# Order edges between the down-projection's weight units and VectorE's additions in a Strassen FFN

## Chip, cores and metric

One core of a Trainium2 chip runs the whole layer as one program. The metric is device time in microseconds (us) of one execution, as the median of several runs. Engines: TensorE (PE; PEld is its weight load), VectorE (DVE), ScalarE (ACT), GpSimd (POOL) and SyncE (SP), whose queue issues most transfers. Each engine takes its instructions in the order of its own queue, and waits at an instruction whose inputs are not there yet.

## What is computed

One layer of a decoder: a modulated norm, an input projection, two kinds of attention, an output projection, and then the FFN, where this change lies:

```python
D_MODEL, SEQ, D_FF = 1024, 1024, 2816
h2 = rmsnorm(x, g_ffn[l]) * (1.0 + sc2) + sh2
gate, up = jnp.split(h2 @ w_gu[l], 2, axis=-1)
x = x + ga2 * ((jax.nn.silu(gate) * up) @ w_down[l])
return rmsnorm(x, g_final)
```

## The kernel before

All arithmetic is float32; a product is made of three matmuls over high and low parts ("h" and "l" tiles) of its operands. The gate and up projections and most of the down-projection use seven products in place of eight (Strassen's scheme), so the operands of a product are sums and differences of blocks.

**The FFN loop** (L1328 to L1357) runs over 22 blocks `f` of 128 columns. In each block `ff_prep` (L1266) loads two pieces of the gate and up weights (L1248, SP), forms four differences of them on GpSimd (L1279, L1280, L1283, L1287), and splits seven operands into high parts on ScalarE (L1241) and low parts on VectorE (L1242). The split operands lie in 20 pages of 512 columns, two for each operand. Seven products follow (`ff_mm`, L1254; twelve matmuls each, L1257 to L1259), in PSUM banks of three kinds: four "mm", two "tp", two "o". VectorE takes the products out of PSUM with seven additions (L1337, L1338, L1340, L1343, L1344, L1347, L1351), ScalarE with one copy (L1336); ScalarE applies silu (L1339, L1348), GpSimd multiplies (L1349, L1352) and sends the two halves of the result to memory (L1350, L1353). The first addition of a block is L1337, into `u2`; L1347, into `u3`, is the sixth.

**The weight units.** Between the blocks the program also prepares the weights of the down-projection for later. There are 40 units (L1295: ten pairs of row blocks by four column pieces). A unit `s` goes through one of three buffers (`wslot`, L1298; tiles `mr0`, `mr1` and `f2`, which the trace shows as mr and f). Its steps: two loads on SP (L1305); two multiplications by the gate on VectorE (L1323, 128x256 each); a store of three of its four parts on SP (L1324); four subtractions in place on GpSimd (L1314 to L1317, 128x128 each), which must wait until that store has read the buffer; a store of the result on SP (L1318); and then the buffer is free for unit `s + 3`.

`w_step(s)` (L1308) writes down three things: the load of unit `s + 1`, the subtractions and second store of unit `s - 1`, and the multiplications and first store of unit `s`. The loop calls `w_step(2f - 2)` ahead of the block's products and `w_step(2f - 1)` behind them, so that units 0 and 1 stand in the text of block 1, units 38 and 39 in that of block 20, and the subtractions of unit 39 in that of block 21. `w_load(0)` stands at the end of block 0.

**What sets the order.** The text of the program is not the order of the queues. When the program is complete, a planner runs it against a time model of its own (`schedule_with_timeline_sim`, L1581): at each step an engine takes, among the instructions that the model says are ready, the one of highest priority, which is the one that stands first in the text (`tc.high_priority` moves some ahead). So an instruction whose inputs are ready early goes into its engine's queue early, however late it stands in the text. The order so found is fixed, and on the chip each engine keeps to it.

**Around the loop.** Ahead of it, `normed`, `turned` and `combined` (L1166 to L1223) make the operands of the FFN, with the last matmuls of the output projection (L367 to L369), transposes (L1187) and splits (L1160, L1161). Behind it stands the down-projection (L1362 on), which reads the units' results back from memory (`w_quarter`, L1408).

Of the kernel before, what the change touches and what calls it, by code (L numbers as in the profile page):

```python
# [15 lines left out]
OP = mybir.AluOpType  # L16
# [52 lines left out]
def hybrid_block(ctx, tc, x, c, w_ada, b_ada, g_attn, w_in, kv_norm_g, w_uk, w_uv, w_out, g_ffn,  # L69
                 w_gu, w_down, g_final, lnm, out, dbg=None):  # L70
    nc = tc.nc
    V, A, G, PE = nc.vector, nc.scalar, nc.gpsimd, nc.tensor

    def pool(stack, name, bufs=1, side=None, **kw):
        if kw.get("space") is None:
            kw["reuse_waits"] = "tile"
        return stack.enter_context(tc.tile_pool(name=name, bufs=bufs, side=side, **kw))
# [18 lines left out]
    def mm_tile(tag="mm"):  # L96
        return ps["pool"].tile([P, 512], F32, name=tag, tag=tag, bufs=ps[tag])
# [498 lines left out]
    for i in range(6):  # L596
        f = 1.0 if i < NV else 2.0
# [546 lines left out]
    def quarters(at, names):  # L1144
        return {n: [at.tile([P, 4, 512], F32R, name=f"A{n}{x}") for x in "hl"] for n in names}

    qA = quarters(pool(qr_ctx, "qR"), ("11", "S2"))
# [103 lines left out]
    def ahead(n):  # L1251
        return tc.high_priority(n) if n else nullcontext()

    def ff_mm(w, a, tag):  # L1254
        p = mm_tile(tag)
        for k in range(4):
            PE.matmul(p, w[1][:, k], a[0][:, k], start=(k == 0), stop=False)  # L1257
            PE.matmul(p, w[0][:, k], a[0][:, k], start=False, stop=False)  # L1258
            PE.matmul(p, w[0][:, k], a[1][:, k], start=False, stop=(k == 3))  # L1259
        return p  # L1260

    def u_tile():
        nu[0] += 1
        return us[nu[0] % 6]

    def ff_prep(f):  # L1266
        b11, b21 = ff_w(f * P)
        b12, b22 = ff_w(DFF + f * P)
        t1, t2, t3, t4 = tsum
        if f == 0:  # L1270
            V.tensor_tensor(t1, b12, b11, op=OP.subtract)
            w1 = page_split(t1)
            V.tensor_tensor(t2, b22, t1, op=OP.subtract)
            G.tensor_tensor(t4, b21, t2, op=OP.subtract)
            w4 = page_split(t4)
            w11 = page_split(b11)
        else:
            w11 = page_split(b11)
            G.tensor_tensor(t1, b12, b11, op=OP.subtract)  # L1279
            G.tensor_tensor(t2, b22, t1, op=OP.subtract)  # L1280
        w2 = page_split(t2)
        w21 = page_split(b21)
        G.tensor_tensor(t3, b22, b12, op=OP.subtract)  # L1283
        w3 = page_split(t3)
        if f > 0:
            w1 = page_split(t1)
            G.tensor_tensor(t4, b21, t2, op=OP.subtract)  # L1287
            w4 = page_split(t4)
        w22 = page_split(b22)
        return w11, w21, w1, w2, w3, w4, w22  # L1290
# [7 lines left out]
    def wslot(s):  # L1298
        return wbuf[s % 3].rearrange("p (u r c) -> p u r c", u=2, r=2), wbuf[s % 3].rearrange("p (a c) -> p a c", c=P)

    def w_load(s):
        if s < len(units):
            j, h = units[s]
            for i, u in enumerate((1, 0)):
                nc.sync.dma_start(wslot(s)[0][:, i], wdn[2 * j:2 * j + 2, :, u * 512 + h * P:u * 512 + h * P + P]  # L1305
                                  .rearrange("r p c -> p r c"))

    def w_step(s):  # L1308
        w_load(s + 1)
        if 1 <= s <= len(units):  # L1310
            j, h = units[s - 1]
            b = wslot(s - 1)[1]
            b12, b22, b11, b21 = [b[:, i] for i in range(4)]
            G.tensor_tensor(b11, b12, b11, op=OP.subtract)  # L1314
            G.tensor_tensor(b12, b22, b12, op=OP.subtract)
            G.tensor_tensor(b22, b22, b11, op=OP.subtract)
            G.tensor_tensor(b21, b21, b22, op=OP.subtract)  # L1317
            nc.sync.dma_start(spill_w[j][:, 3:7, h * P:h * P + P], b)  # L1318
        if s < len(units):
            j, h = units[s]  # L1320
            for i, u in enumerate((1, 0)):
                v = wslot(s)[0][:, i]
                V.tensor_tensor(v, v, gate2[:, u:u + 1, h * P:h * P + P].to_broadcast([P, 2, P]), op=OP.mult)  # L1323
            nc.sync.dma_start(spill_w[j][:, 0:3, h * P:h * P + P], wslot(s)[1][:, 1:4])  # L1324
# [3 lines left out]
    for f in range(NF):  # L1328
        with ahead(PF if f == 0 else 0):
            w11, w21, w1, w2, w3, w4, w22 = ff_prep(f)  # L1330
        if f:
            w_step(2 * f - 2)
        x_, u2, u3, u5 = [u_tile() for _ in range(4)]
        if f == 0:
            p5, p4 = ff_mm(w1, qA["S1"], "tp"), ff_mm(w4, qA["22"], "o")
        A.activation(x_, ff_mm(w11, qA["11"], "mm"), AF.Copy)  # L1336
        V.tensor_tensor(u2, ff_mm(w2, qA["S2"], "tp"), x_, op=OP.add)  # L1337
        V.tensor_tensor(x_, ff_mm(w21, qA["12"], "mm"), x_, op=OP.add)  # L1338
        A.activation(x_, x_, AF.Silu)  # L1339
        V.tensor_tensor(u3, ff_mm(w3, qA["S3"], "mm"), u2, op=OP.add)  # L1340
        if f > 0:
            p5 = ff_mm(w1, qA["S1"], "tp")
        V.tensor_tensor(u5, p5, u3, op=OP.add)  # L1343
        V.tensor_tensor(u2, p5, u2, op=OP.add)  # L1344
        if f > 0:
            p4 = ff_mm(w4, qA["22"], "o")
        V.tensor_tensor(u3, p4, u3, op=OP.add)  # L1347
        A.activation(u3, u3, AF.Silu)  # L1348
        G.tensor_tensor(u5, u3, u5, op=OP.mult)  # L1349
        G.dma_start(spill_g[f][:, :512], u5)  # L1350
        V.tensor_tensor(u2, ff_mm(w22, qA["S4"], "mm"), u2, op=OP.add)  # L1351
        G.tensor_tensor(u2, x_, u2, op=OP.mult)  # L1352
        G.dma_start(spill_g[f][:, 512:], u2)  # L1353
        if f:
            w_step(2 * f - 1)
        else:
            w_load(0)  # L1357
    qa_ctx.close()


# [224 lines left out]
```

## Time and profile before

| what | us |
| --- | --- |
| median of 3 runs (lowest, highest) | 1448.02 (1444.91, 1451.93) |
| the profiled execution | 1453.67 |
| its span, from the first to the last instruction | 1451.8 |
| PE busy in the span | 1305.5 (90%) |
| VectorE busy | 1027.8 (71%) |
| GpSimd busy | 667.1 (46%) |
| ScalarE busy | 591.6 (41%) |

Matmuls overlap in the pipeline, so busy time of PE says little of its speed; how many matmuls fall into a stretch says more. The FFN's first matmul (L1257) starts at 746.6 us of the span, the first addition of its last block (L1337) at 1205.2. In the rows further on, a group of instructions is given by line, engine, operation, output and input; "idle before" is time in which the engine stood still ahead of that instruction, with what ended the wait behind the arrow.

### The profile page before, as it was taken

Reading aid. Unit: us, or ns where it says so; the run is one execution under the profiler, and the core shown is the slowest. Engines: PE = TensorE matmul, PEld = TensorE weight load, DVE = VectorE, ACT = ScalarE, POOL = GpSimd, SP = SyncE. Lnnn points to the kernel's source line nnn. Section 1 sums busy time; section 2 is a strip of 40 time slices with the busy share of each in tenths; the row PEclk is TensorE's granted clock in tenths of the full one; section 3 lists DMA queues with packets and bytes.
Section 4 is the critical chain, followed back from the end, with each engine's and each line's share of the span. In section 5 each row is a group of like instructions: output and inputs, shape, how many; then the busy total and the mean of one; then the engine's idle time right before and its main releaser. Section 6 shows DMA issues by size and latency. Waiting matters only on the chain. (4 is left out here: it accounts for less than half of the span.)

```text
span 1451.8 us, 20937 instructions
## 1 busy us (share of the span) xinstructions
PE 1305.5 (90%) x7477; PEld 1038.0 (71%) x7477; DVE 1027.8 (71%) x1831; ACT 591.6 (41%) x1218; POOL 667.1 (46%) x591
## 2 busy tenths in 40 slices
PE   2999898999878899999849987989999999999995
PEld 0566776898656677787737865767888888787884
DVE  4136899999887566744998556558555555989897
ACT  3435556462446566613653222223333322333344
POOL 1650311314320498223689676768544442312445
PEclk9999898999889999999969999999999999999998
DMA  9723124333411443273546556565222228444404
GB/s 241 232 78 112 30 66 126 97 90 95 124 51 53 134 150 106 89 216 122 164 145 173 169 169 183 172 184 164 87 88 80 87 88 297 167 155 152 151 1 116
DMA packets 196222, 188.85 MB, mean 130 GB/s; under 512 B 12755, under 2 KB 154900, under 8 KB 196118
## 3 DMA queue, kind: packets, MB, share of 16 engines
q1 hardware_dynamic: 185360, 166.27, 38.3%
q0 software_dynamic: 4672, 15.73, 2.9%
q10 hardware_dynamic: 6086, 5.52, 1.5%
q8 instruction: 59, 0.97, 0.3%
q14 instruction: 45, 0.37, 0.1%
HBM read 134.00 MB, written 52.95 MB: 129 GB/s over the span
## 5 line engine op out<-in xcount | busy, mean ns | idle before, releaser
L1242 DVE TENSOR_TENSOR wo<-f,wo 128x512 fp32r<-128x512 f32 x124 | 116.8, 945 | 20.8 <-ACT wo L1241 19.8
L1241 ACT ACTIVATE wo<-f 128x512 fp32r<-128x512 f32 x124 | 75.5, 625 | 118.5 <-PE mm L1259 40.0
L367 PE MATMUL mm<-hh,wl 128*128 128x512 f32 (+2 forms) x288 | 111.6, 389 | 0.0
L368 PE MATMUL mm<-hh,wh 128*128 128x512 f32 (+2 forms) x288 | 111.2, 387 | 0.0
L369 PE MATMUL mm<-hl,wh 128*128 128x512 f32 (+2 forms) x288 | 108.2, 385 | 0.0
L215 POOL TENSOR_SCALAR wh<-wraw 128x1024 fp32r<-128x1024 f32 (+1 forms) x20 | 20.3, 1033 | 133.9 <-PE mm L369 83.7
L1323 DVE TENSOR_TENSOR mr<-mr,ga 128x256 f32<-128x256 f32 x54 | 32.6, 621 | 62.1 <-DMA mr<-in_w_down_dram 46.0
L216 POOL TENSOR_TENSOR wl<-wraw,wh 128x1024 fp32r<-128x1024 f32 (+1 forms) x22 | 52.6, 2412 | 29.8 <-ACT ry L144 29.7
L367 PEld LDWEIGHTS mm<-hh,wl 128*128 128x128 f32 (+1 forms) x288 | 54.4, 189 | 15.2 <-issue 2.8
L369 PEld LDWEIGHTS mm<-hl,wh 128*128 128x128 f32 (+1 forms) x288 | 53.7, 188 | 13.9 <-issue 2.2
L368 PEld LDWEIGHTS mm<-hh,wh 128*128 128x128 f32 (+1 forms) x288 | 54.6, 189 | 11.6 <-issue 1.2
L367 PE MATMUL mm<-wo,wo 128*128 128x512 f32 x148 | 58.0, 392 | 1.9 <-DVE wo L1417 1.9
L368 PE MATMUL mm<-wo,wo 128*128 128x512 f32 x148 | 57.6, 389 | 0.0
L1339 ACT ACTIVATE f<-f 128x512 f32<-128x512 f32 x22 | 13.9, 633 | 106.9 <-DVE f L1338 106.6
L369 PE MATMUL mm<-wo,wo 128*128 128x512 f32 x148 | 57.2, 390 | 0.0
L794 ACT ACTIVATE ttB<-ttB,mn 128x128 f32<-128x128 f32 (+7 forms) x64 | 49.1, 768 | 15.5 <-DVE mn L790 14.9
L367 PE MATMUL mm<-wo,ml 128*128 128x512 f32 x128 | 51.0, 398 | 3.0 <-POOL ml L1110 1.6
L763 PE MATMUL tp<-ident,ttB 128*128 128x128 f32 x288 | 44.3, 298 | 10.2 <-ACT ptB L809 9.7
L621 DVE TENSOR_SCALAR_CACHE_REDUCE score<-kl,sc 128x1024 bf16<-128x1024 uint16 (+2 forms) x48 | 52.3, 1140 | 0.0
L621 DVE TENSOR_SCALAR_CACHE_REDUCE score<-ka,sc 128x768 bf16<-128x768 int16 (+2 forms) x48 | 52.3, 1139 | 0.0
L1493 POOL TENSOR_TENSOR f<-f,f 128x1536 f32<-128x1536 f32 (+1 forms) x5 | 21.5, 4295 | 65.7 <-DVE wo L1417 33.5
L425 DVE SCALAR_TENSOR_TENSOR score<-rl,wi,score 128x512 f32<-128x512 f32 (+2 forms) x70 | 48.1, 742 | 4.2 <-ACT rl L419 3.3
(473 smaller groups left out, 4320.6 us busy)
## 6 DMA issues: line engine op xcount, KB each, us to landing
f<-in_w_gu_dram SPq DMA_DIRECT2D x44, 512.0 KB, 4.2
spg<-f POOLq DMA_DIRECT2D x44, 256.0 KB, 3.1
wraw<-in_w_in_dram SPq DMA_DIRECT2D x21, 512.0 KB, 3.9
f<-spw SPq DMA_DIRECT2D x35, 256.0 KB, 3.1
more<-spw SPq DMA_DIRECT2D x35, 256.0 KB, 3.1
f<-spg SPq DMA_DIRECT2D x33, 256.0 KB, 3.3
va<-in_w_ada_dram SPq DMA_DIRECT2D x16, 512.0 KB, 4.6
wlm<-in_w_ada_dram SPq DMA_DIRECT2D x32, 256.0 KB, 2.7
```

Source lines behind the costliest of these rows:

```text
L216: G.tensor_tensor(lo, raw, hi.bitcast(F32), op=OP.subtract)
L367: PE.matmul(p, al, bh, start=(j == 0), stop=False)
L368: PE.matmul(p, ah, bh, start=False, stop=False)
L369: PE.matmul(p, ah, bl, start=False, stop=(j == n - 1))
L425: V.scalar_tensor_tensor(sc, rl, w, sc, op0=OP.mult, op1=OP.add)
L621: V.tensor_scalar(mask(t, u), keys[:, seg[t]], z[:, i:i + 1], 0.0, op0=OP.is_lt, op1=OP.add, accum_out=cnt[:, i:i + 1])
L763: pe_last[0] = op(*args, **kw)
L794: A.activation(tts[e], tts[e], AF.Exp, bias=mns[e][:, j:j + 1], scale=-1.0, accum_out=st["lt", half][:, i, e:e + 1])
L1241: A.activation(h_, src, AF.Copy)
L1242: V.tensor_tensor(l_, src, h_.bitcast(F32), op=OP.subtract)
L1323: V.tensor_tensor(v, v, gate2[:, u:u + 1, h * P:h * P + P].to_broadcast([P, 2, P]), op=OP.mult)
L1493: eng.tensor_tensor(*v, op=op)
```

## The change

`w_step(2f - 2)` is moved from ahead of the block's products to just behind the first addition, and `w_step(2f - 1)` from the end of the block to just behind the sixth. Both calls (and `w_load(0)` in block 0) now stand in `tc.issue_after(done.ins)`. That draws an order edge, with no wait on a semaphore, from the named addition to each instruction in the call that runs on the same engine as the addition: the planner may put that instruction only behind the addition. The addition is on VectorE, so the edges bind the two multiplications of a unit (L1323) and nothing else; the loads and stores on SP and the subtractions on GpSimd get none. In block 0 the call holds no instruction of VectorE.

```diff
     for f in range(NF):
         with ahead(PF if f == 0 else 0):
             w11, w21, w1, w2, w3, w4, w22 = ff_prep(f)
-        if f:
-            w_step(2 * f - 2)
         x_, u2, u3, u5 = [u_tile() for _ in range(4)]
         if f == 0:
             p5, p4 = ff_mm(w1, qA["S1"], "tp"), ff_mm(w4, qA["22"], "o")
         A.activation(x_, ff_mm(w11, qA["11"], "mm"), AF.Copy)
-        V.tensor_tensor(u2, ff_mm(w2, qA["S2"], "tp"), x_, op=OP.add)
+        done = V.tensor_tensor(u2, ff_mm(w2, qA["S2"], "tp"), x_, op=OP.add)
+        if f:
+            with tc.issue_after(done.ins):
+                w_step(2 * f - 2)
         V.tensor_tensor(x_, ff_mm(w21, qA["12"], "mm"), x_, op=OP.add)
...
-        V.tensor_tensor(u3, p4, u3, op=OP.add)
+        done = V.tensor_tensor(u3, p4, u3, op=OP.add)
+        with tc.issue_after(done.ins):
+            w_step(2 * f - 1) if f else w_load(0)
         A.activation(u3, u3, AF.Silu)
...
         G.dma_start(spill_g[f][:, 512:], u2)
-        if f:
-            w_step(2 * f - 1)
-        else:
-            w_load(0)
```

## Rows read from the trace of the kernel before

**Rows 1.** Stretches: busy us (count) of PE, PEld, DVE, ACT, POOL; clock, DMA share, GB/s

```profile
767.00:986.00 219.00, 195.57 (x800) 153.44 (x798) 135.44 (x196) 52.09 (x94) 158.75 (x205) 0.97 0.61 177
1029.00:1205.00 176.00, 176.00 (x762) 143.07 (x761) 89.42 (x123) 56.10 (x88) 82.61 (x72) 1.00 0.27 86
```

**Rows 2.** Waits of PE, 767 to 1205 us: total us, times, longest

```profile
PE mm L1257 <- DVE f L1351: 9.5, 5, 3.1
PE tp L1257 <- DVE f L1344: 8.4, 4, 4.0
PE tp L1257 <- DVE f L1337: 3.3, 2, 2.1
```

**Rows 3.** Groups on VectorE, 767 to 986 us: busy us, mean ns | idle before

```profile
L1242 DVE TENSOR_TENSOR wo<-f,wo 128x512 fp32r<-128x512 f32 x53 | 50.5, 955 | 2.5 <-ACT wo L1241 2.5
L1323 DVE TENSOR_TENSOR mr<-mr,ga 128x256 f32<-128x256 f32 x44 | 25.0, 587 | 61.8 <-DMA mr<-in_w_down_dram 45.7 <-issue 5.7 <-POOL mr L1316 3.6
L1323 DVE TENSOR_TENSOR f<-f,ga 128x256 f32<-128x256 f32 x23 | 16.7, 744 | 19.1 <-DMA f<-in_w_down_dram 14.6 <-POOL mr L1315 2.3 <-POOL f L1352 1.7
```

**Rows 4.** The chain that ended last, one stretch of it: start, us, what

```profile
857.95 4.77 DMA mr<-in_w_down_dram
862.75 0.44 DVE mr L1323
863.20 0.37 SPq L1324
863.66 2.50 DMA spw<-mr
866.23 3.74 DMA mr<-in_w_down_dram
870.05 0.36 DVE mr L1323
```

**Rows 5.** Timeline of VectorE: start, us, instruction

```profile
709.99 0.43 DVE L1323 TENSOR_TENSOR mr<-mr,ga 128x256 f32<-128x256 f32 x1
...
767.17 0.68 DVE L1337 TENSOR_TENSOR f<-tp,f 128x512 f32<-128x512 f32 x1
...
984.30 1.03 DVE L1323 TENSOR_TENSOR mr<-mr,ga 128x256 f32<-128x256 f32 x2 [1.49 <-DMA mr<-in_w_down_dram]
...
1028.92 0.69 DVE L1337 TENSOR_TENSOR f<-tp,f 128x512 f32<-128x512 f32 x1 [0.89 <-PE tp L1259]
...
1039.97 0.69 DVE L1347 TENSOR_TENSOR f<-o,f 128x512 f32<-128x512 f32 x1 [0.84 <-PE o L1259]
...
1205.18 0.68 DVE L1337 TENSOR_TENSOR f<-tp,f 128x512 f32<-128x512 f32 x1
```

**Rows 6.** Stretches of 20 us, columns as in rows 1

```profile
780.00:800.00 20.00, 20.00 (x88) 16.27 (x87) 18.13 (x22) 7.08 (x14) 19.17 (x21) 1.00 0.50 145
...
860.00:880.00 20.00, 17.10 (x73) 13.25 (x71) 9.63 (x16) 5.50 (x10) 12.70 (x18) 1.00 0.56 166
...
1020.00:1040.00 20.00, 20.00 (x88) 16.26 (x87) 10.79 (x17) 6.18 (x10) 9.35 (x9) 1.00 0.34 105
```

**Rows 7.** Stretches ahead of the loop: all engines, then L1323 alone (DVE, clock, DMA)

```profile
720.00:740.00 20.00, 5.41 (x21) 3.86 (x20) 19.89 (x34) 12.43 (x29) 12.80 (x14) 0.66 0.59 177
740.00:760.00 20.00, 12.19 (x36) 8.92 (x36) 20.00 (x23) 8.61 (x18) 18.15 (x16) 0.57 0.30 86
...
720.00:740.00 20.00, 3.05 (x5) 0.66 0.59 177
740.00:760.00 20.00, 4.78 (x6) 0.57 0.30 86
```

**Rows 8.** Waits of PE ahead of the loop, 640 to 760 us

```profile
PE tp L1187 <- DVE rm L157: 9.4, 1, 9.4
PE tp L1187 <- DVE f L1180: 8.8, 2, 6.1
```

**Rows 9.** Groups on GpSimd, 767 to 986 us, columns as in rows 3

```profile
L1280 POOL TENSOR_TENSOR f<-f,f 128x512 f32<-128x512 f32 x10 | 14.1, 1408 | 0.0
L1317 POOL TENSOR_TENSOR mr<-mr 128x128 f32<-128x128 f32 x22 | 13.9, 635 | 0.5
```

**Rows 10.** Groups on VectorE, 1029 to 1205 us, columns as in rows 3

```profile
L1242 DVE TENSOR_TENSOR wo<-f,wo 128x512 fp32r<-128x512 f32 x47 | 36.5, 777 | 15.5 <-ACT wo L1241 14.7
L1338 DVE TENSOR_TENSOR f<-mm,f 128x512 f32<-128x512 f32 x9 | 6.2, 692 | 12.8 <-PE mm L1259 12.8
```

## The prediction

> **What bounds the kernel now.** I read the stretches first, because the 90% of PE in the table is an average. In the second half of the loop 762 matmuls take 176 us, 0.231 us each, and PE is never idle; in the first half 800 matmuls take 219 us [rows 1]. At the later pace those 800 need 800 x 0.231 = 184.8 us, so the first half loses 34.2 us. The second view says who holds PE back: its longest waits are all for VectorE's additions, which empty the PSUM banks [rows 2]. The third says why these additions are late. A group's idle time stands behind the bar: ahead of the units' multiplications VectorE stood still for 61.8 + 19.1 = 80.9 us, mostly until the unit's load had landed [rows 3]. VectorE takes its queue in order, so the additions behind such a multiplication waited too. The chain shows the same from the other side: for long stretches it runs through a unit's buffer (load, multiplication, store, and the load of the next unit) and not through the products [rows 4].
>
> Why do loads and multiplications meet so closely? The planner took each multiplication as soon as its model had the load there. The first runs at 710 us, 57 us ahead of the first addition of the FFN, the last at 984 us, about half-way through the loop, and after that there are none [rows 5]. In the first half 67 multiplications, 33.5 units, pass in 219 us, one in 6.5 us [rows 1, 3]; with three buffers, one buffer turns round in 19.6 us. The units run at the pace of their own buffers, and the products wait for them.
>
> **The change part by part.** No instruction or transfer is added or removed. What moves: 80 multiplications, bound by the edges; and, free to follow, 80 loads, 80 stores and 160 subtractions.
>
> *The stall in the first half.* The edges allow two units in each of blocks 1 to 20. A late block lasts (1205.18 - 1028.92) / 9 = 19.6 us from first addition to first addition, and the sixth addition comes 11.1 us after the first [rows 5]; so the places are 11.1 and 8.5 us apart, and one buffer turns round in 1.5 blocks, 29.4 us. The chain of a buffer needed 19.6 us, waits in the queues included. That leaves about 10 us between a load's landing and the addition that its multiplication stands behind. Loads and subtractions have no edge, so they still start as soon as a buffer is free. I therefore take the waits ahead of L1323 as gone, and with them the 34.2 us. Bounds: all of it (the late blocks show the pace without units) or nothing (waits of the same length at the new places).
>
> *The ramp ahead of the loop.* Between 720 and 760 us VectorE is busy for 39.9 of 40 us, 7.8 us of it with units [rows 7], and PE waits for VectorE [rows 8]. These multiplications move into the loop, and the subtractions that follow them on GpSimd, busy 30.95 us there [rows 7], go too. What the path gets back is between nothing (other work of VectorE, such as weight splits, fills the gap) and 7.8 us. I take 5: VectorE hardly stands still there, so most of what is taken from it shortens the way to the products.
>
> *The units' work in the later blocks.* This is the price. A late block holds 89.42 / 9 = 9.9 us of VectorE and 82.61 / 9 = 9.2 us of GpSimd [rows 1]. Two units add four multiplications of 0.59 to 0.74 us [rows 3], at most 3.0 us, and eight subtractions of about 0.64 us [rows 9], 5.1 us. That makes 12.9 and 14.3 us of 19.6, and both stay below PE. Queued behind the first pair are addition L1338 and low parts L1242, and behind the second low parts and the last addition, L1351; whoever waits for these is PE, for a bank or for a page. An addition in the late blocks finds VectorE idle (12.8 us in nine times, 1.4 us each, ahead of L1338 [rows 10]), and a pair of 1.2 to 1.5 us just fits; what does not fit is taken up by the eight banks for seven products. One stretch already shows units and products together: from 780 to 800 us VectorE is busy for 18.1 us and GpSimd for 19.2, with units in both, and PE still runs 88 matmuls, as many as from 1020 to 1040 us, where no unit is left; from 860 to 880 us it runs 73 [rows 6]. So the work itself costs PE nothing; the waits do. I still take 4 us of friction, 0.2 us a block, between 0 and 10 (0.5 us a block), because the fixed order couples four queues.
>
> *The other queues.* SP's loads of gate and up weights stand behind stores that wait for multiplications and subtractions; the number of these does not change, and they come further apart. GpSimd gets a unit's subtractions among the four differences for the next block and the two products of this one; the 5.1 us fit in the 10.4 us that a late block leaves it. The last unit's store comes in block 21, ahead of any load of the down-projection that needs it, so I cost this at nothing; the cover is the first chunk, which needs units 0 to 11 alone.
>
> *A rule weighed.* VectorE's low parts take 0.955 us on average beside the units and 0.777 us without [rows 3, 10]: GpSimd slows VectorE, by 0.18 us. In the Trainium skill, "SBUF — State Buffer", section "Who interferes with whom", says that a VectorE instruction with two SBUF inputs and a GpSimd instruction that reads SBUF block each other for the whole instruction. The trace agrees in direction, but not with a full block each time. By the rows the sum stays as above, since 0.18 us for eleven such instructions a block is 2 us of VectorE's slack; a full block each time gives the last rival below.
>
> *Sum.* -34.2 - 5 + 4 = -35.2 us. The profiled execution took 1453.67 us, so it would take 1418.5; that is 5.65 us above the median of the runs shown, 1448.02, from which the same sum gives 1412.8. I forecast 1413 us.
>
> **The rivals.**
>
> *Part of the stall stays.* The planner's model may still place a load on SP behind a store that is late on the chip, so that some multiplications wait. For it: such waits are longer on the chip than the planner thought, 2.4 us each for mr (45.7 us in 19). Against it: 10 us of room. If half of the 34.2 us stays, the time is 1448.0 - 17 = 1431 us; I give this 1427 to 1440.
>
> *The wait returns at every place.* If all 40 units wait as they do now, 80.9 / 33.5 = 2.4 us each, then at today's rate (34.2 us of PE for 80.9 us of VectorE's waits) PE loses 40 x 1.0 = 41 us in place of 34: with the ramp's 5 us back, 1450 us, no change. It decides at a buffer's turn of 29.4 us: only if a store, a subtraction or a load waits some 10 us more than now.
>
> *The change does nothing.* If the multiplications ran behind these additions already, the edges would be empty: 1448 us. The first at 710 us speaks against it [rows 5].
>
> *Slower: VectorE becomes the bound in every block.* Place: blocks 1 to 20. Without blocking, a block of VectorE is seven additions at 0.69, seven low parts at 0.78 and four multiplications at 0.59, 12.6 us. If each of the eleven instructions with two SBUF inputs waited out a whole instruction of GpSimd (1.41 us for a difference beside a low part, 0.64 for a subtraction beside a multiplication [rows 9]), that is 7 x 1.41 + 4 x 0.64 = 12.4 us more: 25.0 us against PE's 19.6, 5.4 us over, 108 us in 20 blocks. After the gains of 39 us: 1517 us. It decides where the added wait passes (19.6 - 12.6) / 11 = 0.64 us per instruction; the first half shows 0.18 with GpSimd busy for 158.75 of 219 us [rows 1], about the share it would have now (14.3 of 19.6). The Trainium skill's rule above, taken in full, is this case.
>
> **How the numbers follow.** Forecast 0.73, its own range 1403 to 1427 (a gain between 24 and 42, from the ramp's 0 to 7.8 and friction of 10 to 0, and some 3 us either way as the runs before scatter). Part of the stall stays 0.12. The wait returns 0.08, the change does nothing 0.02: both no change. VectorE as the bound 0.05. A measurement of this kernel tells about 0.5%, 7.2 us, from no change: faster is below 1440.8. So faster is 0.73 + 0.12 = 0.85, same 0.10, slower 0.05. The range runs from 1401, the bounds at their best, up into the partial case, to 1434; it leaves out the upper end of that case and the other three, some 0.2 in all.
>
> **What would show it right or wrong.** Multiplications in pairs behind L1337 and L1347 in blocks 1 to 20, none ahead of the loop; idle time ahead of L1323 below 15 us in place of 80.9 in the first half; about 88 matmuls in each 20 us of the whole loop; the first addition of the last block some 35 us earlier than 1205; the chain through the products and no longer through mr and f; the first addition of block 0 some 5 us earlier than 767. I am wrong if VectorE still waits for loads at L1323, if low parts average above 1.4 us, if PE now waits for splits or differences (L1242, L1279 to L1287), or if the down-projection takes longer than before and gives the gain back.

## The result and the profile after

| | before | after |
| --- | --- | --- |
| median of runs, us (lowest to highest) | 1448.67 (1444.91 to 1451.93) | 1405.61 (1404.11 to 1407.86) |
| the profiled execution, us | 1453.67 | 1404.39 |
| its span, us | 1451.8 | 1402.6 |
| first addition of block 0 starts at, us | 767.2 | 751.1 |
| first addition of block 21 starts at, us | 1205.2 | 1155.1 |
| between the two | 438.0 | 404.0 |
| from there to the end of the span | 246.6 | 247.5 |

The ratio is 0.9705, with a 95% interval of 0.9676 to 0.9733: 43 us faster. The forecast was 1413, the range 1401 to 1434. The span of the profiled execution shrank by 49 us, more than the medians, since the profiled execution of before lay 5 us above its median. By the table 16 of these 49 us lie ahead of the loop and 34 in it; behind it nothing changed (+0.9).

The stretches of the loop, columns as in [rows 1], from the kernel after:

```profile
767.00:986.00 219.00, 219.00 (x947) 177.96 (x946) 157.75 (x205) 69.48 (x113) 161.38 (x179) 1.00 0.52 153
986.00:1140.00 154.00, 154.00 (x666) 125.21 (x665) 104.83 (x142) 49.44 (x80) 113.55 (x127) 1.00 0.54 160
```

In the same 219 us PE now starts 947 matmuls, not the 800 of [rows 1], at 0.231 us each, the pace that the late blocks had before; and it keeps this pace while GpSimd is busy for 74% of the stretch.

Not all of the 34 us of the loop were waits. From the first addition of block 0 to that of block 21 (us, PE busy with its count, clock, DMA share, GB/s), before and after:

```profile
767.17:1205.18 438.01, 413.73 (x1742) 0.98 0.46 137
751.06:1155.05 403.99, 403.99 (x1747) 1.00 0.52 153
```

But for five records of some 1745 the matmuls are as many. Before, PE stood idle for 24.3 of the 438.0 us; the other 9.7 us (413.73 - 403.99) are matmuls that took longer, most of them in stretches where the granted clock had fallen. One such stretch of before:

```profile
855.00:860.00 5.00, 4.46 (x13) 0.66 0.53 148
```

PE had been busy for only 2.48 of the 5 us before it, and the matmuls that follow its wait of 3.06 us come 0.43 us apart, not 0.23, until the clock is back from the lower of its two levels (1.2 GHz) to the higher (2.4 GHz). A wait of PE cost more here than its own length.

Groups on VectorE between 780 and 1140 us, after (mean ns, then idle time ahead), against [rows 3, 10]:

```profile
L1242 DVE TENSOR_TENSOR wo<-f,wo 128x512 fp32r<-128x512 f32 x103 | 107.3, 1041 | 35.8 <-ACT wo L1241 35.3
L1323 DVE TENSOR_TENSOR mr<-mr,ga 128x256 f32<-128x256 f32 x48 | 28.1, 625 | 0.0
L1323 DVE TENSOR_TENSOR f<-f,ga 128x256 f32<-128x256 f32 x26 | 15.2, 625 | 0.0
```

The 80.9 us ahead of L1323 are gone to the last tenth. The low parts (L1242) average 1.04 us here (0.97 in e11, the same kernel once more) against 0.955 beside the units before, and nobody pays for it: PE waits for nothing between 767 and 1155 us. The places of the multiplications on VectorE's timeline (the first addition is now line 1335, the sixth 1348):

```profile
751.06 0.68 DVE L1335 TENSOR_TENSOR f<-tp,f 128x512 f32<-128x512 f32 x1
...
881.16 1.04 DVE L1323 TENSOR_TENSOR mr<-mr,ga 128x256 f32<-128x256 f32 x2
892.32 1.18 DVE L1323 TENSOR_TENSOR mr<-mr,ga 128x256 f32<-128x256 f32 x2
...
900.69 1.48 DVE L1323 TENSOR_TENSOR f<-f,ga 128x256 f32<-128x256 f32 x2
911.75 1.02 DVE L1323 TENSOR_TENSOR mr<-mr,ga 128x256 f32<-128x256 f32 x2
...
1155.05 0.68 DVE L1335 TENSOR_TENSOR f<-tp,f 128x512 f32<-128x512 f32 x1
```

A buffer is used at 881.2 and again, three units on, at 911.8 us: 30.6 us. In between SP's queue shows how long its chain takes:

```profile
886.00 0.45 SPq L1324 DMA_DIRECT2D spw<-mr  x1
...
893.24 0.37 SPq L1318 DMA_DIRECT2D spw<-mr  x1
895.54 0.92 SPq L1305 DMA_DIRECT2D mr<-in_w_down_dram  x2
```

The first store is issued at 886.0, the second at 893.2, the loads of the next unit from 895.5 on. Such loads land 2.7 us after they are issued (median of this kernel), so the chain is done after some 17 us, 13 us ahead of the addition that the next multiplication stands behind. That is why nothing waits.

Ahead of the loop (columns as in [rows 7], the kernel after):

```profile
720.00:740.00 20.00, 8.58 (x26) 6.47 (x27) 18.79 (x31) 15.44 (x36) 13.51 (x10) 0.54 0.36 92
740.00:760.00 20.00, 20.00 (x83) 16.14 (x83) 15.95 (x17) 9.13 (x15) 17.09 (x12) 0.95 0.36 106
```

Between 740 and 760 us PE runs 83 matmuls where it ran 36 [rows 7]. This is an earlier start: the FFN's first matmul stands at 734.3 us in place of 746.6, and in both kernels the first matmuls of the FFN meet a granted clock of 0.50 (1.2 GHz), from 730 to 755 us before and from 725 to 740 us after, where PE has had little to do.

### The profile page after: what moved, and what is told of

Read it like the earlier page. It is cut to its first block, busy times and chain, and to the rows that moved or that the text cites. A ratio compares the mean times of both kernels' runs of the same rounds, so it can differ in the third digit from the quotient of the medians.

```text
span 1402.6 us, 20904 instructions
## 1 busy us (share of the span) xinstructions
PE 1292.7 (92%) x7477; PEld 1034.5 (74%) x7477; DVE 1040.1 (74%) x1831; ACT 598.1 (43%) x1218; POOL 679.4 (48%) x591
## 4 chain that ended last, share of the span: by engine, by line
PE 60%; DVE 25%; DMA 4%; issue 4%; ACT 3%; POOL 2%; SPq 1%; DVEq 0%; ACTq 0%; POOLq 0%
DVE score L621 7%; PE mm L1257 6%; PE mm L1258 6%; PE mm L1259 6%; PE mm L367 4%; PE mm L368 4%; PE o L763 4%; PE mm L369 4%; PE mm L763 3%; PE tp L763 3%; PE tp L1259 3%; PE tp L1257 3%; PE tp L1258 3%; DVE score L425 2%; PE o L1257 1%
## 5 line engine op out<-in xcount | busy, mean ns | idle before, releaser
L1242 DVE TENSOR_TENSOR wo<-f,wo 128x512 fp32r<-128x512 f32 x124 | 131.0, 1059 | 39.8 <-ACT wo L1241 39.2
L216 POOL TENSOR_TENSOR wl<-wraw,wh 128x1024 fp32r<-128x1024 f32 (+1 forms) x22 | 52.7, 2415 | 30.6 <-ACT ry L144 30.5
L621 DVE TENSOR_SCALAR_CACHE_REDUCE score<-kl,sc 128x1024 bf16<-128x1024 uint16 (+2 forms) x48 | 52.3, 1140 | 0.0
L369 PE MATMUL mm<-wo,mh 128*128 128x512 f32 x128 | 50.4, 393 | 0.0
L368 PE MATMUL mm<-wo,mh 128*128 128x512 f32 x128 | 50.3, 393 | 0.0
```

The source lines that it names most:

```text
L216: G.tensor_tensor(lo, raw, hi.bitcast(F32), op=OP.subtract)
L368: PE.matmul(p, ah, bh, start=False, stop=False)
L369: PE.matmul(p, ah, bl, start=False, stop=(j == n - 1))
L621: V.tensor_scalar(mask(t, u), keys[:, seg[t]], z[:, i:i + 1], 0.0, op0=OP.is_lt, op1=OP.add, accum_out=cnt[:, i:i + 1])
L1242: V.tensor_tensor(l_, src, h_.bitcast(F32), op=OP.subtract)
```

## The experiments

"First" and "last" are the starts of the first additions of blocks 0 and 21 in one profiled execution; the time is a median of runs, the ratio against the kernel before on the same chip, with its interval.

| run | us | ratio | first | last | between |
| --- | --- | --- | --- | --- | --- |
| e1, text only | 1447.12 | 0.9984 [0.9954, 1.0015] | 770.9 | 1206.3 | 435.4 |
| e2, ramp only | 1440.73 | 0.9937 [0.9919, 0.9956] | 749.3 | 1187.6 | 438.3 |
| e3, pace only | 1417.79 | 0.9783 [0.9742, 0.9823] | 765.7 | 1170.6 | 404.9 |
| e7, e3 again | 1418.11 | 0.9775 [0.9735, 0.9815] | 765.9 | 1169.9 | 404.0 |
| e4, both at the first addition | 1402.65 | 0.9674 [0.9642, 0.9706] | 753.8 | 1157.0 | 403.2 |
| e12, e4 again | 1404.28 | 0.9687 [0.9668, 0.9706] | 754.8 | 1158.0 | 403.2 |
| e11, after again | 1405.72 | 0.9697 [0.9675, 0.9718] | 754.0 | 1158.4 | 404.4 |
| e10, three per block | 1425.43 | 0.9837 [0.9815, 0.9860] | 753.4 | 1175.4 | 422.0 |
| e5, four per block | 1437.11 | 0.9909 [0.9879, 0.9939] | 751.7 | 1189.4 | 437.7 |
| e6, subtractions twice | 1414.07 | 0.9752 [0.9712, 0.9791] | 755.8 | 1167.5 | 411.7 |
| e8, first seven without multiplications | 1412.75 | 0.9732 [0.9690, 0.9774] | 758.4 | 1164.7 | 406.3 |
| e9, first seven without subtractions | 1412.53 | 0.9740 [0.9719, 0.9760] | 761.8 | 1164.4 | 402.6 |

**Is it the edges?** e1 moves the calls and leaves the edges out:

```diff
-            with tc.issue_after(done.ins):
-                w_step(2 * f - 2)
+            w_step(2 * f - 2)
...
-        with tc.issue_after(done.ins):
-            w_step(2 * f - 1) if f else w_load(0)
+        w_step(2 * f - 1) if f else w_load(0)
```

> The calls stand in the text where the change puts them, but without the order edges. Theory (the edges do it, since the planner takes a multiplication as soon as its load is there in its model): the units run ahead again from about 710 us on, some 80 us of idle time stand ahead of L1323, and the time is that of the kernel before, 1443 to 1453 us. Rival (the place in the text, that is, the priority, does it): 1405 to 1415 us.

1447.12 us, no change. What ended the idle time of VectorE ahead of L1323 in this kernel (us, times):

```profile
  DMA mr<-in_w_down_dram: 54.5, 24
  DMA f<-in_w_down_dram: 19.7, 8
```

With three smaller waits that is 80.9 us of idle time, the waits for loads are back [rows 3], and the first multiplication stands at 713.7 us. The move in the text is worth nothing by itself.

**Two gains, taken apart.** e2 keeps the text of before and holds every multiplication behind the first addition of block 0 alone:

```diff
-        if f:
-            w_step(2 * f - 2)
+        if f:
+            with tc.issue_after(start.ins):
+                w_step(2 * f - 2)
...
+        if f == 0:
+            start = done
...
-            w_step(2 * f - 1)
+            with tc.issue_after(start.ins):
+                w_step(2 * f - 1)
```

> The text of before; every multiplication of a unit stands behind the first addition of block 0 and is free from there on. Theory (two separate gains, some 16 us ahead of the loop and 34 us in it): the ramp is as after the change, first addition near 751 us, but the 40 units then run at the pace of their buffers and cost about 1 us each, 41 us in place of 34: 1435 to 1445 us. Rival (what counts is that nothing runs ahead of the loop; in the loop the units' waits are made up for): 1403 to 1412 us.

1440.73 us, in the theory's range. Block 0 starts as early as after the change, and the loop is as long as before. The expected 41 us of loss for 40 units was too much: 438.3 - 404.0 = 34 us, about what 33.5 units cost before.

e3 is the opposite: the first seven units are free, as many as ran ahead of the loop before, and the rest is paced.

```diff
+        if f == 1:
+            for s in range(7):
+                w_step(s)
...
-                w_step(2 * f - 2)
+                w_step(2 * f + 5)
...
-            w_step(2 * f - 1) if f else w_load(0)
+            w_step(2 * f + 6) if f else w_load(0)
```

> The first seven units are free, as before, and run ahead of the loop; the others stand two per block behind the same two additions. Theory (two separate gains): the ramp is that of before, the loop that of after: the first addition of block 0 between 762 and 768 us, no idle time ahead of L1323 in the loop, 1414 to 1424 us. Rival (the 16 us of the ramp were scatter between two profiled executions, or come from the order of other instructions): 1403 to 1410 us.

1417.79 us, in the theory's range, with the start of before (765.7) and the loop of after (404.9). e7 was meant to be another kernel and was e3 unaltered, so it counts as a repeat: 1418.11, 765.9 and 404.0.

> As e3_pace_only, with the subtractions of the first seven units left out (their weights come out wrong); their loads, multiplications and stores stay ahead of the loop. This splits the 15 us that the ramp costs with units in it (first addition of block 0 at 766 us in e3_pace_only, at 751 after the change). Theory (half of it is GpSimd's work, which holds VectorE's instructions with two SBUF inputs): first addition between 756 and 761 us, 5 to 10 us below e3_pace_only. Rival (all of it is VectorE's multiplications): 764 to 768 us, no difference to e3_pace_only.

In medians, then, the pace is worth about 31 us (1449.09, the kernel before on that chip, less 1417.79) and the ramp 12 (1417.8 and 1418.1 against 1405.6 and 1405.7). The start of block 0 scatters by some 3 us between executions of one kernel (751.1 and 754.0 us in the kernel after), so differences of that size in one execution say little.

**What the ramp is made of.** e8 and e9 are e3 with one half of the first seven units' work left out:

```diff
# e8
-                V.tensor_tensor(v, v, gate2[:, u:u + 1, h * P:h * P + P].to_broadcast([P, 2, P]), op=OP.mult)
+                if s >= 7:
+                    V.tensor_tensor(v, v, gate2[:, u:u + 1, h * P:h * P + P].to_broadcast([P, 2, P]), op=OP.mult)
# e9
-            G.tensor_tensor(b11, b12, b11, op=OP.subtract)
+            if s > 7:
+                G.tensor_tensor(b11, b12, b11, op=OP.subtract)
...
```

> As e3_pace_only, with the multiplications of the first seven units left out (their weights come out without the gate); their loads, subtractions and stores stay ahead of the loop. Theory (half of the ramp's 15 us is VectorE's own 8 us of multiplications): first addition between 756 and 761 us, 5 to 10 us below e3_pace_only. Rival (all of it is GpSimd's work): 764 to 768 us. Rival (all of it is VectorE's multiplications): 750 to 754 us.

> As e3_pace_only, with the subtractions of the first seven units left out (their weights come out wrong); e7 was meant to be this and was e3_pace_only over again. Without the first seven units' multiplications (e8) the first addition of block 0 came at 758 us, between the 766 of e3_pace_only and the 751 after the change. Theory (the other half is GpSimd's subtractions, by holding VectorE's instructions with two SBUF inputs and standing ahead of GpSimd's own splits): first addition between 755 and 762 us, 1409 to 1416 us. Rival (the other half is loads and stores, or the planner's order, and the subtractions cost nothing): 764 to 768 us, 1415 to 1422 us.

The first additions of the 22 blocks, one row for each kernel: after "x22" stands their duration in ns (three values), then the start of the first and of the last of them in us. In e2, where no unit lies in the ramp:

```profile
L1338 DVE TENSOR_TENSOR f<-tp,f x22: 676/682/693, 749.3 to 1187.6; 128x512 f32<-128x512 f32 x22
```

In e3, with all the work of seven units in the ramp:

```profile
L1338 DVE TENSOR_TENSOR f<-tp,f x22: 675/692/694, 765.7 to 1170.6; 128x512 f32<-128x512 f32 x22
```

In e8, with the seven units but without their multiplications:

```profile
L1339 DVE TENSOR_TENSOR f<-tp,f x22: 676/692/694, 758.4 to 1164.7; 128x512 f32<-128x512 f32 x22
```

In e9, with the seven units but without their subtractions:

```profile
L1339 DVE TENSOR_TENSOR f<-tp,f x22: 675/692/694, 761.8 to 1164.4; 128x512 f32<-128x512 f32 x22
```

Both expectations hold: leaving out VectorE's half starts block 0 about 7 us earlier, leaving out GpSimd's half 4 us; in medians each gives some 5 us (1412.75 and 1412.53; e3 and e7 together, eight runs from 1412.65 to 1424.01, lie at 1418). So neither "all VectorE" nor "all GpSimd" stands.

The two halves can't simply be added up, though. Busy time of VectorE between 680 and 770 us (busy us and count, then clock, DMA share, GB/s), first in the sixteen low parts L1161, then in the fourteen multiplications of the seven units. In e3:

```profile
680.00:770.00 90.00, 24.22 (x16) 0.81 0.52 160
680.00:770.00 90.00, 10.38 (x14) 0.81 0.52 160
```

In e9, without the subtractions:

```profile
680.00:770.00 90.00, 21.48 (x16) 0.83 0.62 186
680.00:770.00 90.00, 5.50 (x14) 0.83 0.62 186
```

In e8, without the multiplications (low parts only):

```profile
680.00:770.00 90.00, 18.74 (x16) 0.85 0.56 175
```

Without the subtractions the same multiplications take 5.50 us, not 10.38; without the multiplications the low parts are as short as after the change (18.95 us), although all the subtractions are there. And in the kernel before one more wait stands right ahead of block 0's first addition (767.17 us):

```profile
765.23 2.02 DVE L1323 TENSOR_TENSOR f<-f,ga 128x256 f32<-128x256 f32 x2 [3.37 <-DMA f<-in_w_down_dram]
```

VectorE stood still for 3.37 us until a unit's load had landed (3.3 and 3.7 us in e3 and e7), and the addition behind it, whose last matmul had ended at 763.6 us, started 3.5 us late. Leaving out either half removes this wait: e8 has no such multiplications, and in e9 the last of them starts at 747.7 us. So the two halves share a part, and how the 12 us divide among multiplications, subtractions, this wait and the planner's other rearrangements was not measured.

**How near may the places be?** e4 puts both units behind the first addition, e10 a third one behind the sixth, e5 two behind each:

```diff
# e4, and e10 with w_step(3 * f - 3) and w_step(3 * f - 2)
             with tc.issue_after(done.ins):
                 w_step(2 * f - 2)
+                w_step(2 * f - 1)
...
# e10
-            w_step(2 * f - 1) if f else w_load(0)
+            w_step(3 * f - 1) if f else w_load(0)
# e5: w_step(4 * f - 4), w_step(4 * f - 3) first, then w_step(4 * f - 2), w_step(4 * f - 1)
```

> Both units of a block stand behind the first addition, so that with three buffers a buffer turns round partly in one block, 19.5 us, and not in 29. Theory as predicted (a buffer's chain needs 19.6 us): loads land about when they are wanted or some us late, idle time ahead of L1323 between 20 and 80 us in all, 1409 to 1426 us. Rival (the 19.6 us of before held waits in the queues; the chain itself is some 13 us): no idle time, 1403 to 1409 us.

> Four units per block, two behind each of the two additions, so that all are done in ten blocks; a buffer is wanted again after 9 to 20 us, 14.6 on average. Theory (what decides is whether a buffer's chain of load, multiplication, store, subtractions, store and load, some 12 to 17 us by its pieces, fits between two places): it no longer fits, idle time of 50 us or more returns ahead of L1323, the ten blocks are longer than 19.4 us, 1415 to 1440 us. Rival (only the order counts: a multiplication right behind an addition does no harm at any pace): no idle time, 1403 to 1410 us.

> Two units behind the first addition, one behind the sixth: one unit in 6.5 us, the pace of the first half before the change, but each buffer has one whole block of 19.4 us from use to use, at places fixed by edges. Theory (what costs time is a place nearer than the chain of a buffer, not the pace): no idle time of note ahead of L1323 (under 10 us), loop of 403 to 407 us from the first addition of block 0 to that of block 21, 1402 to 1409 us. Rival (the pace of 6.5 us is what the buffers cannot keep): idle time of 50 us and more, 1425 to 1445 us.

e4 missed the theory's range by 6 us on the fast side, and the rival had it right: no idle time ahead of L1323, although a buffer comes round in 20.2 us (multiplications from 883.98 us on, then from 904.18 us on). There the two stores go out together, and the next loads at 896.6 us, 12.6 us after the multiplications; landed 3 us later, the chain takes some 16 us. e5, in its range, waits again (60.3 + 23.1 us ahead of L1323 between 770 and 1160 us).

e10 missed the theory, and it is the run that teaches most: fixed places, one whole block for each buffer, and yet 1425 us. VectorE in one block of e10, with the wait in brackets:

```profile
869.05 0.68 DVE L1335 TENSOR_TENSOR f<-tp,f 128x512 f32<-128x512 f32 x1
875.44 0.42 DVE L1323 TENSOR_TENSOR mr<-mr,ga 128x256 f32<-128x256 f32 x1 [5.72 <-DMA mr<-in_w_down_dram]
...
878.51 1.03 DVE L1323 TENSOR_TENSOR mr<-mr,ga 128x256 f32<-128x256 f32 x2 [0.64 <-DMA mr<-in_w_down_dram]
...
892.31 0.68 DVE L1335 TENSOR_TENSOR f<-tp,f 128x512 f32<-128x512 f32 x1
898.77 0.76 DVE L1323 TENSOR_TENSOR mr<-mr,ga 128x256 f32<-128x256 f32 x2 [5.78 <-DMA mr<-in_w_down_dram]
```

and SP's queue in the same block:

```profile
882.90 0.37 SPq L1318 DMA_DIRECT2D spw<-f  x1
883.31 1.06 SPq L1324 DMA_DIRECT2D spw<-mr  x2
...
893.58 0.92 SPq L1318 DMA_DIRECT2D spw<-mr  x2
895.95 0.89 SPq L1305 DMA_DIRECT2D mr<-in_w_down_dram  x2
```

The two units are multiplied by 879.5 us, but their stores go out at 883.3: they stand in SP's queue behind the second store of the third unit of the block before (882.90), which waits for that unit's subtractions on GpSimd. Then the eight subtractions, between GpSimd's work for the products, last until the store at 893.6, and the loads go out at 896. From multiplication to multiplication that is 23 us, and the block lasts 23.3 us (869.05 to 892.31) in place of 19.4. So a chain has no length of its own: 16 to 17 us in e4 and after the change, 23 with a third unit in the same block, because the units stand in each other's way on SP and GpSimd. The pace counts as well as the places, and the rival was right.

**Is the units' work hidden?** e6 does each of the four subtractions twice:

```diff
             G.tensor_tensor(b11, b12, b11, op=OP.subtract)
             G.tensor_tensor(b12, b22, b12, op=OP.subtract)
             G.tensor_tensor(b22, b22, b11, op=OP.subtract)
             G.tensor_tensor(b21, b21, b22, op=OP.subtract)
+            G.tensor_tensor(b11, b12, b11, op=OP.subtract)
+            G.tensor_tensor(b12, b22, b12, op=OP.subtract)
+            G.tensor_tensor(b22, b22, b11, op=OP.subtract)
+            G.tensor_tensor(b21, b21, b22, op=OP.subtract)
```

> As after the change, with each of a unit's four subtractions on GpSimd done twice (the down-projection's weights come out changed). GpSimd is busy for 14.3 of 19.4 us in a block after the change, and would be for some 19.5. Theory (the units' work is hidden as long as each engine's sum stays below PE's block of 19.4 us): GpSimd now just reaches the block, so blocks 1 to 20 get longer by 0.2 to 1.5 us each, 1409 to 1436 us; PE waits for splits or differences. Rival 1 (slack between the engines hides even this): 1403 to 1409 us. Rival 2 (VectorE's instructions with two SBUF inputs are held by GpSimd and VectorE becomes the bound): over 1436 us, low parts (L1242) above 1.4 us on average.

1414.07 us, 8.5 us above the kernel after: the theory's range, but not its way. Two stretches of e6, columns as in [rows 1], and two waits of VectorE between 770 and 1160 us:

```profile
1000.00:1100.00 100.00, 100.00 (x433) 81.26 (x432) 68.56 (x93) 27.19 (x50) 91.68 (x120) 1.00 0.52 152
...
1180.00:1200.00 20.00, 17.07 (x66) 13.37 (x66) 13.23 (x19) 2.00 (x2) 4.76 (x4) 0.91 1.01 374
```

```profile
DVE f L1348 <- DMA spg<-f: 48.4, 15, 4.5
DVE f L1345 <- POOL f L1359: 28.1, 16, 2.4
```

With GpSimd busy for 92% of the time VectorE waits for its results and for the stores that it issues, and PE still runs its 433 matmuls in 100 us: the banks cover it. (The 411.7 us between the first additions hold 1780 matmuls, not 1747, at the same pace.) It is lost at the ends: block 0 starts 2 to 5 us later (755.8 against 751.1 and 754.0), and where the loop hands over to the down-projection PE runs 66 matmuls in 20 us, not 88. The low parts average 1.02 us; nothing like a bound on VectorE shows.

**A better version?** e4 had the lower median by 3 us, so it was run again beside the kernel after:

> The kernel after the change, unaltered, beside e12 and the kernel before on one chip. Both theories: 1403 to 1409 us, first addition of block 0 at 749 to 754 us.

> e4_both_at_first again, to see whether it beats the kernel after. Theory (PE bounds the loop in both, so that there is nothing left to gain from the places): within 3 us of e11. Rival (the shorter multiplications, 0.42 in place of 0.62 us, free VectorE and give 3 us or more): 1399 to 1403 us, and at least 3 us below e11.

1405.72 and 1404.28 us, intervals overlapping: no difference that these runs can tell. Low parts and multiplications are shorter in e4 (0.42 us for a multiplication of mr against 0.62), and since PE bounds the loop in both, it brings nothing. No version beat the kernel after.

## Why the prediction was right, and where not

*What bounds the kernel, and the stall in the first half*: right. The 34.2 us worked out from the count of matmuls came back as 34.0 (438.0 - 404.0) in the profiled executions, and e3 and e1 show that the edges, and the pace that they set, do it. The prediction put all of it down to waits; 24.3 us were PE's waits, 9.7 us matmuls at a lower clock behind them. A count of matmuls holds both, so the sum came out right.

*"The chain of a buffer needed 19.6 us, ... about 10 us between a load's landing and the addition"*: right in its conclusion (13 us after the change), wrong as a property of the chain. It took 16 to 17 us with two units in a block (after, e4), 23 with three (e10). The 19.6 us were the pace of that crowd, not a need.

*The ramp*: this term was mis-sized. I took 5 us, bounded by the 7.8 us of multiplications between 720 and 760 us; the runs show 12 in medians, and block 0 starts 13 to 16 us earlier, not 5. The step that failed is the upper bound, in three ways. Its window ended 7 us ahead of the first addition: all fourteen multiplications ahead of it took 10.7 us before (10.38 in e3), and the wait of 3.37 us for the last of their loads was not in the sum. The low parts L1161 beside them got no price, and took 24.2 us before against 18.95 after. And GpSimd's subtractions were named as leaving too, and given no price: without them (e9) the multiplications take half as long, and the time falls by some 5 us in the median.

*Friction*: 4 us taken, none found in the profiled execution, where PE runs at its pace throughout. The late blocks of before had already run at the pace that all blocks now have, and the slack of eight banks and twenty pages covers 14.3 us of GpSimd (265.15 us between 780 and 1140, by 360 / 19.4 = 18.6 blocks), as forecast, and 13.5 us of VectorE, a little over the 12.9 forecast. In medians the stall and the friction can't be told apart: together they gave 31 us, where 34.2 - 4 = 30.2 was forecast.

So of the 8 us by which the gain was larger (35 forecast, 43 measured) the ramp holds 7. That 1405.6 still lies in the range is owed to its lower end, which took friction at nothing and the ramp at its bound of 7.8 us (1406 us before scatter). The ramp's bound was too low; that the range held all the same is luck there.

*The rivals*: "part of the stall stays" and "the wait returns at every place" did not come true at two units a block; e10 and e5 show the second with three and four. "VectorE becomes the bound" fell: low parts average 0.97 to 1.04 us after the change (GpSimd at 74% in the profile shown), and 1.02 with GpSimd at 92%, far from 1.4. "The change does nothing" holds only without the edges (e1).

## What to carry to other kernels

A planner that places each instruction as soon as its model has the inputs there puts background work at places with no slack on the chip, and an engine that takes its queue in order makes the foreground pay for each late load. Tie background work to foreground instructions at an even pace, just as much per block as the block's helpers can finish; one unit more per block made the units late for each other (e10: 20 us). Where background work is taken out of a crowded stretch, price it on every engine that it leaves, with its waits and up to the instruction that the next stage needs, not only on the one that this stage waits for.

## What the runs showed of the hardware

Short VectorE instructions with two SBUF inputs can take much longer than one instruction of GpSimd beside them. Before the change, VectorE and GpSimd ahead of the loop:

```profile
715.71 5.65 DVE L1161 TENSOR_TENSOR AS3l<-f,AS3h 128x512 fp32r<-128x512 f32 x1
```

```profile
715.78 0.47 POOL L1315 TENSOR_TENSOR mr<-mr 128x128 f32<-128x128 f32 x1
716.20 1.29 POOL L1210 TENSOR_TENSOR f<-f 128x512 f32<-128x512 f32 x1
717.45 0.46 POOL L1316 TENSOR_TENSOR mr<-mr 128x128 f32<-128x128 f32 x1
717.87 1.28 POOL L1161 TENSOR_TENSOR A12l<-f,A12h 128x512 fp32r<-128x512 f32 x1
719.12 0.45 POOL L1317 TENSOR_TENSOR mr<-mr 128x128 f32<-128x128 f32 x1
719.54 1.28 POOL L1215 TENSOR_TENSOR f<-f,f 128x512 f32<-128x512 f32 x1
```

The low part took 5.65 us (0.68 at best after the change) and ended at 721.4, just after the last of six GpSimd instructions that follow each other without a gap (720.8), three of them subtractions of a unit. Without the subtractions (e9) the longest of its kind took 3.16 us, with them (e3) 5.65. In the kernel after, with no unit there, the same is seen on an instruction of 128x1 that takes 0.21 us elsewhere, beside GpSimd instructions that end at 705.8 us:

```profile
701.63 4.21 DVE L162 SCALAR_TENSOR_TENSOR rt<-ry,rm 128x1 f32<-128x1 f32 x1
```

The Trainium skill, "SBUF — State Buffer", section "Who interferes with whom", has one of the two block the other for its whole instruction; by these times, and it is read from times alone, the block can span a run of GpSimd instructions. It is not what makes the subtractions dear by itself: it occurs without them too, and in e8, with all of them, the low parts are short. Where the products run, low parts averaged 1.04 us: of 129 between 780 and 1140 us after the change one took 3.4 us, and all but one of the others less than 1.9.
